# Two sums over partitions on two 32-column quarters of the PE array, in one step of a hybrid diffusion backbone

## The chip, the core and the metric

The kernel runs on one core of a Trainium2 chip. The metric is the device time of one execution in microseconds (us). A core has five engines with queues of their own: PE (TensorE, matrix products), DVE (VectorE), ACT (ScalarE), POOL (GpSimd) and SP (SyncE), which here issues every data transfer. PE loads a stationary operand (its weights, an operand in the array) and streams a moving operand past it; the result goes to PSUM, which has 128 partitions in banks of 2 KB per partition. An engine works off its queue in order, and semaphores make it wait for others.

## The reference, cut to what matters

One layer: a modulated RMSNorm, a mixer (gated DeltaNet heads beside a chunked gMLP), a gated residual, a second modulated RMSNorm, a squared-ReLU MLP, a gated residual, and a final norm. There are 128 context rows and 2048 latent rows of width 1024. The modulation is what the change touches:

```python
def modulation(cond, w_mod_l, b_mod_l):
    m = jax.nn.silu(cond) @ w_mod_l + b_mod_l          # (1,1024) @ (1024,6144) + (6144)
    return jnp.split(m[:, None, :], N_MOD, axis=-1)    # sh1, sc1, ga1, sh2, sc2, ga2
...
    mod_ctx = modulation(c_ctx[None, :], w_mod[l], b_mod[l])
...
    mod_lat = modulation(c, w_mod[l], b_mod[l])
```

So two conditioning rows (context and latent) are multiplied by the same 1024 x 6144 matrix, and the same bias row is added to both.

## The kernel before

The program is written as Python that issues instructions; a scheduler then sets the order on each engine (`schedule_with_timeline_sim=True`: it replays the program against its own cost table and picks what is ready), so an edit in one place can move instructions elsewhere. Three stages follow each other:

- Stage 1 (to about 430 us): projections of q, k and v for six blocks of tokens. Products `pj<-kH,wH`, `pj<-kL,wH` and `pj<-kH,wL` (lines 220 to 222) are one exact product in three parts of high and low halves. Transposes and small products for the scan lie between them, on the banks `pt`.
- Stage 2 (to about 1220 us): the scan over chunks in both directions, the gMLP and the output projection.
- Stage 3 (from about 1240 us to the end): the MLP, products on the banks `f`.

The modulation is worked out in twelve pieces of 512 columns. The first ones have code of their own: pieces 0 to 3 in `mod_columns`, piece 4 in `split_mod_steps`. Pieces 5 to 9 run in stage 1 and pieces 10 and 11 in stage 3, in `mod_steps(jc, ...)`, which the change edits. For each of eight chunks of 128 matrix rows it loads `raw` (128 x 512, line 235), and DVE multiplies it by the conditioning column of that chunk and adds it to an accumulator, once for each conditioning row `c` (lines 254 and 256, `acc`, in stage 3 `macc`). Then each of the two accumulators must be summed over its 128 partitions. This is `total()`: PE does it with a stationary operand `pick` that holds ones, DVE adds the bias row (line 274), and SP stores the two rows to `mod_d` in DRAM (line 275), from where later stages read them. `bias()` loads the bias (line 265).

In `total()` before, `pick` has two slices of 2 columns: a column of ones at place 0 or at place 1, zeros beside it. Both products write the same two PSUM rows, the second one onto the first.

The accumulators have one buffer each, and so has the row `mrow`: DVE can start on the next piece's `acc` only when PE has read the last one, and the bias of the next piece can be loaded only when the last row's store has landed. In stage 1 the steps of `mod_steps` are dealt out between the projections by `MOD_STEPS` and `interleave`; in stage 3 by the table `mods`.

A product of two f32 operands, such as `pm<-acc,pick`, shows in the trace as two weight loads and two matmuls: the hardware does it in two passes. A total of two products thus has four passes, and the seven totals have 28.

One other place is used in the prediction. In the scan, lines 1224 and 1228 put 64 x 64 products on quarters of the array: both contract the partitions `ra` (64 of the 128), line 1224 with its result on the partitions `ra`, line 1228 on the other 64, `rb`:

```python
T.matmul(py[ra, h, :], g["X"][ra, h, ra], pm[ra, h, 0:64], start=True, stop=True)   # L1224
...
T.matmul(px[rb, h, :], pm[ra, h, 0:64], g["X"][ra, h, ra], start=True, stop=True)   # L1228
```

On PE's queue, at the first pair of scan units (about 500 us), four of the one stand ahead of four of the other, each after its weight load:

```order
L1224 LDWEIGHTS X
L1224 MATMUL pd<-R,X 64x64
L1224 LDWEIGHTS X
L1224 MATMUL pd<-R,X 64x64
L1224 LDWEIGHTS X
L1224 MATMUL pd<-R,X 64x64
L1224 LDWEIGHTS X
L1224 MATMUL pd<-R,X 64x64
L1228 LDWEIGHTS R
L1228 MATMUL pd<-X,R 64x64
```

This place is the same in both kernels; the rows are shown because the trace has the start of each of these products.

Of the kernel before, what the change touches and what calls it, by code (L numbers as in the profile page):

```python
# [8 lines left out]
F32 = mybir.dt.float32  # L9
# [5 lines left out]
ALU = mybir.AluOpType  # L15
# [3 lines left out]
P = 128  # L19
# [43 lines left out]
def hybrid_step(  # L63
# [7 lines left out]
    V, A, G, T = nc.vector, nc.scalar, nc.gpsimd, nc.tensor  # L71
    load = nc.sync.dma_start
    store = nc.sync.dma_start
# [18 lines left out]
    mod_d = dp.tile([2, 6 * D], F32, name="mod_d")  # L92
# [73 lines left out]
    smp = ctx.enter_context(tc.tile_pool(name="small", bufs=4, reuse_waits="tile"))  # L166
# [40 lines left out]
    def w512(name, dt=F32):  # L207
        return wp.tile([P, 512], dt, tag="w", name=name)
# [12 lines left out]
            T.matmul(ps, lh, rl, start=False, stop=False, skip_group_check=more)  # L221
            T.matmul(ps, ll, rh, start=False, stop=last and i == n - 1, skip_group_check=more)  # L222

    pick = smp.tile([P, 2, 2], F32, tag="pick", name="pick", bufs=1)
    V.memset(pick, 0.0)
    V.memset(pick[:, 0, 0:1], 1.0)
    V.memset(pick[:, 1, 1:2], 1.0)

    def mod_steps(jc, pool, stage=None, psum=None, pair=None):

        u = {}

        def fetch_raw(k):
            raw = stage() if stage else sp.tile([P, 512], F32, tag="raw", name="raw")
            load(out=raw, in_=w_mod[0, k * P : (k + 1) * P, jc * 512 : (jc + 1) * 512])
            return raw

        def f(k):
            if pair:
                if k == 0:  # L240
                    u[0], u[1] = fetch_raw(0), fetch_raw(1)
                raw = u.pop(k)
                if k + 2 < KT:
                    u[k + 2] = fetch_raw(k + 2)
            else:
                raw = fetch_raw(k)
            if k == 0:
                if pair:
                    u["acc"] = pair()
                else:  # L250
                    u["acc"] = [pool.tile([P, 512], F32, tag=f"acc{c}", name="acc", bufs=1) for c in range(2)]
            for c, acc in enumerate(u["acc"]):
                if k == 0:
                    V.tensor_scalar_mul(acc, raw, scond[:, k, c : c + 1])
                else:
                    V.scalar_tensor_tensor(out=acc, in0=raw, scalar=scond[:, k, c : c + 1], in1=acc,
                                           op0=ALU.mult, op1=ALU.add)
            if k == KT - 1 and not pair:
                total()
            elif k == KT - 1:  # L260
                u["row"] = pair()[0][0:2, :]
                bias(u["row"])

        def bias(row):
            load(out=row, in_=b_mod[0:1, jc * 512 : (jc + 1) * 512].to_broadcast([2, 512]))

        def total():
            ps = (psum or pm1)()
            for c, acc in enumerate(u["acc"]):
                T.matmul(ps[0:2, :], pick[:, c, :], acc, start=c == 0, stop=c == 1)  # L270
            row = u["row"] if pair else pool.tile([2, 512], F32, tag="mrow", name="mrow", bufs=1)
            if not pair:
                bias(row)
            V.tensor_tensor(out=row, in0=ps[0:2, :], in1=row, op=ALU.add)
            store(out=mod_d[:, jc * 512 : (jc + 1) * 512], in_=row)

        return [lambda k=k: f(k) for k in range(KT)] + ([total] if pair else [])

    head = {}

    with ExitStack() as ph:
# [8 lines left out]
        def pt():  # L290
            return ppt.tile([P, 512], F32, tag="pt", name="pt", bufs=3)
# [93 lines left out]
        ps = pt()  # L385
# [328 lines left out]
        def second_mods():  # L714
# [8 lines left out]
            for cd in range(2):  # L723
                V.scalar_tensor_tensor(out=a2[:, cd, :], in0=pc4[:, cd, 1, :], scalar=1.0, in1=vec[:, 24:32],
                                       op0=ALU.add, op1=ALU.mult)

        mods = [st for jc in range(4, 10) for st in (split_mod_steps(jc) if jc == 4 else mod_steps(jc, p1))]
        blk, xs_, cols = prep_block(0)
        for st in xs_:
# [30 lines left out]
        for bi in range(len(BLOCKS)):  # L760
# [8 lines left out]
            for n, (gi, h) in enumerate(order):  # L769
                u = us[n] if bi == 0 and n < 3 else feature_tile(blk, bi, gi, h)  # L770
# [156 lines left out]
    with ExitStack() as ph:  # L927
# [554 lines left out]
        for i, u in enumerate(units):  # L1482
# [3 lines left out]
            c = i % 2  # L1486
# [107 lines left out]
    def bank():  # L1594
        return psq.tile([P, 512], F32, tag="f", name="f", bufs=8)
# [19 lines left out]
    class Unit:  # L1615
# [6 lines left out]
        def load(self, i, kh):  # L1622
            for q in range(2):
                self.raw[i, kh, q] = r = w512("raw")
                r0, c0 = kh * 512 + q * 256, self.jp * 512 + i * 256
                load(out=r.rearrange("p (a c) -> p a c", a=2),
                     in_=w_ff1[0, r0 : r0 + 256, c0 : c0 + 256].rearrange("(a p) c -> p a c", p=P))
# [130 lines left out]
    acc = {}  # L1758
# [210 lines left out]

    junk16 = smp.tile([P, 512], BF16, tag="junk16", name="junk16", bufs=1)  # L1970
    mods = [st for jc in range(10, 12) for st in mod_steps(jc, wp, lambda: w512("mraw"), bank, mrow)]
    mods = {half + 28 + 4 * j: st for j, st in enumerate(mods)}

# [8 lines left out]
    for p, (o, n, m) in enumerate(seq):  # L1982
        u = units[n]
# [37 lines left out]
    for m, (n, i, u, q) in enumerate(todo):  # L2021
# [6 lines left out]
        if q == 0:  # L2028
            ps = bank()
# [80 lines left out]
```

## Time and profile before

| | |
|---|---|
| median of 3 runs | 2579.31 us (2576.31 to 2580.29) |
| span of the profiled execution, first to last instruction | 2574.7 us (the profile gives no other time of it) |
| PE busy | 2542.1 us, 99% |
| DVE busy | 1781.9 us, 69% |
| ACT busy | 1192.5 us, 46% |
| DMA | 579.77 MB, 225 GB/s on average |

The span leaves out what lies around the execution; the median of the runs is 4.6 us longer. A profile row of a group gives the line, engine, operation, result and operands by the program's names, count, and durations in ns; a row of the timeline gives start, length, and what ran, with "x4" for four in a row. A matmul's duration in the trace includes its way through the array, and the next one starts before it ends; so what a stream of matmuls costs is read from start to start.

### The profile page before, as it was taken

What the parts mean: (1) busy time and instruction counts of PE and PEld (TensorE: products, weight loads), DVE (VectorE), ACT (ScalarE), POOL (GpSimd) and SP (SyncE); (2) the same over time, 40 slices, a digit from 0 to 9 for tenths busy, and PEclk for the clock granted to TensorE, in tenths of its full rate; (3) what the DMA queues carried; (4) which work ended last, traced back from release to release, by engine and by line L of the source; (5) the groups of instructions that cost most, each with busy time, mean ns of one, the idle gap of its engine ahead of it and who ended that gap; (6) DMA issues with size and microseconds to landing.
All of it is one profiled execution on the core that took longest, in us unless ns stands there. A gap on an engine that the chain in (4) does not pass through costs nothing.

```text
span 2574.7 us, 43713 instructions
## 1 busy us (share of the span) xinstructions
PE 2542.1 (99%) x15296; PEld 2134.4 (83%) x15296; DVE 1781.9 (69%) x3524; ACT 1192.5 (46%) x2758; POOL 313.9 (12%) x512
## 2 busy tenths in 40 slices
PE   8999999999999999999999999999999999999998
PEld 4999999788888778888888888888888888888887
DVE  5777746666667788885587887677674445675874
ACT  4755555554545556763355553333243333243441
POOL 3112112222222233331000000000000000000000
PEclk9999999999999999999999999999999999999999
DMA  8966637755555758896778798445599878786773
GB/s 293 297 221 208 197 118 231 235 165 168 165 168 177 229 185 261 280 311 209 268 219 252 214 292 284 140 144 155 177 298 310 279 261 301 238 258 212 232 251 107
DMA packets 533859, 579.77 MB, mean 225 GB/s; under 512 B 35500, under 2 KB 366684, under 8 KB 530054
## 3 DMA queue, kind: packets, MB, share of 16 engines
q1 hardware_dynamic: 533638, 576.98, 70.5%
q8 instruction: 120, 1.97, 0.3%
q14 instruction: 101, 0.83, 0.1%
HBM read 397.62 MB, written 179.22 MB: 224 GB/s over the span
## 4 chain that ended last, share of the span: by engine, by line
PE 55%; DVE 1%; issue 1%; DMA 0%; ACT 0%; POOL 0%; SPq 0%; DVEq 0%; POOLq 0%; ACTq 0%
PE f L220 17%; PE f L221 17%; PE f L222 17%; PE pj L220 1%; PE pj L222 1%; PE pj L221 1%; PE f L856 0%; PE pd L992 0%; PE pd L1096 0%; PE pd L1097 0%; DMA gr<-g_d 0%; PE pm L1418 0%; DMA x<-in_x_sample_dram 0%; PE pd L1060 0%; PE f L270 0%
## 5 line engine op out<-in xcount | busy, mean ns | idle before, releaser
L220 PE MATMUL f<-hop,zH 128*128 128x512 f32 x960 | 373.2, 389 | 0.0
L222 PE MATMUL f<-hop,zL 128*128 128x512 f32 x960 | 373.1, 389 | 0.0
L221 PE MATMUL f<-hop,zH 128*128 128x512 f32 x960 | 373.1, 389 | 0.0
L220 PE MATMUL f<-hop,wH 128*128 128x512 f32 x896 | 351.5, 393 | 0.0
L221 PE MATMUL f<-hop,wH 128*128 128x512 f32 x896 | 348.9, 390 | 0.0
L222 PE MATMUL f<-hop,wL 128*128 128x512 f32 x896 | 344.3, 390 | 0.0
L1604 ACT CAST zH<-zraw 128x512 fp32r<-128x512 f32 x240 | 146.5, 620 | 296.0 <-DMA zraw<-s_d 92.7
L1598 DVE TENSOR_TENSOR zL<-zraw,zH 128x512 fp32r<-128x512 f32 x240 | 162.1, 687 | 72.7 <-ACT zH L1604 61.6
L220 PEld LDWEIGHTS f<-hop,zH 128*128 128x128 f32 x960 | 180.3, 188 | 37.3
L222 PEld LDWEIGHTS f<-hop,zL 128*128 128x128 f32 x960 | 180.2, 188 | 37.3
L221 PEld LDWEIGHTS f<-hop,zH 128*128 128x128 f32 x960 | 180.2, 188 | 37.3
L222 PEld LDWEIGHTS f<-hop,wL 128*128 128x128 f32 x896 | 168.2, 188 | 35.6
L220 PEld LDWEIGHTS f<-hop,wH 128*128 128x128 f32 x896 | 168.5, 188 | 34.1 <-issue 0.9
L221 PEld LDWEIGHTS f<-hop,wH 128*128 128x128 f32 x896 | 168.6, 188 | 32.2
L222 PE MATMUL pj<-kH,wL 128*128 128x386 f32 (+2 forms) x568 | 190.6, 335 | 0.0
L220 PE MATMUL pj<-kH,wH 128*128 128x386 f32 (+2 forms) x568 | 189.1, 336 | 0.3 <-DVE kH L487 0.3
L221 PE MATMUL pj<-kL,wH 128*128 128x386 f32 (+2 forms) x568 | 189.3, 333 | 0.0
L178 POOL TENSOR_TENSOR r<-rsq,nhalf 128x1 f32<-128x1 f32 (+1 forms) x38 | 22.3, 587 | 1352.4 <-DVE rsq L177 1352.4
L1751 ACT CAST wH<-s 128x512 fp32r<-128x512 f32 x96 | 58.9, 620 | 172.8 <-DVE s L1598 157.3
L537 DVE SCALAR_TENSOR_TENSOR cv<-pj,vec,cv 128x384 f32<-128x384 f32 (+2 forms) x164 | 87.1, 538 | 58.4 <-ACT cv L534 57.0
L220 PEld LDWEIGHTS pj<-kH,wH 128*128 128x128 f32 x568 | 107.1, 189 | 4.9 <-issue 4.4
L221 PEld LDWEIGHTS pj<-kL,wH 128*128 128x128 f32 x568 | 107.4, 189 | 0.6
(408 smaller groups left out, 5729.3 us busy)
## 6 DMA issues: line engine op xcount, KB each, us to landing
zraw<-z_d SPq DMA_DIRECT2D x212, 256.0 KB
raw<-in_w_ff_dram SPq DMA_DIRECT2D x128, 256.0 KB
hop<-hop_d SPq DMA_DIRECT2D x28, 1024.0 KB
z_d<-c SPq DMA_DIRECT2D x96, 256.0 KB
zraw<-s_d SPq DMA_DIRECT2D x96, 256.0 KB
raw<-in_w_mod_dram SPq DMA_DIRECT2D x80, 256.0 KB
r<-in_w_ff_dram SPq DMA_DIRECT2D x80, 256.0 KB
s_d<-s SPq DMA_DIRECT2D x64, 256.0 KB
```

The source lines that it names most:

```text
L178: G.tensor_tensor(out=out, in0=t[:np_, :n], in1=nhalf[:np_, :n], op=ALU.pow)
L220: T.matmul(ps, lh, rh, start=first and i == 0, stop=False, skip_group_check=more)
L221: T.matmul(ps, lh, rl, start=False, stop=False, skip_group_check=more)
L222: T.matmul(ps, ll, rh, start=False, stop=last and i == n - 1, skip_group_check=more)
L537: V.scalar_tensor_tensor(out=cv[:, o : o + m], in0=ps[:, s + sh : s + sh + m], scalar=convw[:, w, j : j + 1], in1=cv[:, o : o + m], op0=AL ...
L1598: V.tensor_tensor(out=out, in0=a, in1=b, op=op)
L1604: A.copy(h, src)
L1751: A.copy(h, s2)
```

## The change

`pick` becomes one tile of 32 columns with ones in column 0. The two products of `total()` use the same `pick`. The one for conditioning row 0 goes to columns 0 to 31 of the array with its result on PSUM partitions 0 to 31, the other to columns 32 to 63 with its result on partitions 32 to 63, each a product of its own (`start` and `stop` both set) instead of the second being added to the first. The sums then lie on partitions 0 and 32 instead of 0 and 1, so the bias load, the bias add and the store, one instruction each before on two rows, become two each on one row.

```diff
-    pick = smp.tile([P, 2, 2], F32, tag="pick", name="pick", bufs=1)
+    pick = smp.tile([P, 32], F32, tag="pick", name="pick", bufs=1)
     V.memset(pick, 0.0)
-    V.memset(pick[:, 0, 0:1], 1.0)
-    V.memset(pick[:, 1, 1:2], 1.0)
+    V.memset(pick[:, 0:1], 1.0)
...
-                u["row"] = pair()[0][0:2, :]
+                u["row"] = pair()[0][0:33, :]
                 bias(u["row"])
 
+        def one(c):
+            return slice(32 * c, 32 * c + 1)
+
         def bias(row):
-            load(out=row, in_=b_mod[0:1, jc * 512 : (jc + 1) * 512].to_broadcast([2, 512]))
+            for c in range(2):
+                load(out=row[one(c), :], in_=b_mod[0:1, jc * 512 : (jc + 1) * 512])
 
         def total():
             ps = (psum or pm1)()
             for c, acc in enumerate(u["acc"]):
-                T.matmul(ps[0:2, :], pick[:, c, :], acc, start=c == 0, stop=c == 1)
-            row = u["row"] if pair else pool.tile([2, 512], F32, tag="mrow", name="mrow", bufs=1)
+                T.matmul(ps[32 * c : 32 * c + 32, :], pick, acc, start=True, stop=True)
+            row = u["row"] if pair else pool.tile([33, 512], F32, tag="mrow", name="mrow", bufs=1)
             if not pair:
                 bias(row)
-            V.tensor_tensor(out=row, in0=ps[0:2, :], in1=row, op=ALU.add)
-            store(out=mod_d[:, jc * 512 : (jc + 1) * 512], in_=row)
+            for c in range(2):
+                V.tensor_tensor(out=row[one(c), :], in0=ps[one(c), :], in1=row[one(c), :], op=ALU.add)
+                store(out=mod_d[c : c + 1, jc * 512 : (jc + 1) * 512], in_=row[one(c), :])
```

The scheduler's order changes with it. PE and ACT have the same instructions in both kernels; between about 150 and 360 us several hundred of them stand in another order, and after that PE's order is the same again to the end. Three places matter for the prediction (line numbers after the change are up to 4 higher below the edit: L270, L274, L275 and L265 become L273, L278, L279 and L268).

PE, the third of the five totals of stage 1. Before, it follows the second one after 282 instructions of PE:

```order
L221 MATMUL pj<-kL,wH 128x386
L222 MATMUL pj<-kH,wL 128x386
L270 MATMUL pm<-acc,pick 2x512 x2
L549 MATMUL pt<-ident,x_3215 128x128 x3
L220 MATMUL pj<-kH,wH 128x386
```

After, it stands 141 instructions behind the second one, between other projections:

```order
L583 MATMUL pt<-ident,kn 128x128 x3
L222 MATMUL pj<-kH,wL 128x386
L273 MATMUL pm<-acc,pick 32x512 x2
L220 MATMUL pj<-kH,wH 128x386
L221 MATMUL pj<-kL,wH 128x386
```

It has moved forward by half the way; its two products still stand side by side, as they do in the first, second and fourth total and in the two of stage 3.

PE, the fifth total. Before:

```order
L222 MATMUL pj<-kH,wL 128x386
L270 MATMUL pm<-acc,pick 2x512 x2
L220 MATMUL pj<-kH,wH 128x386
```

After, the first of its two products stands here:

```order
L222 MATMUL pj<-kH,wL 128x386
L273 MATMUL pm<-acc,pick 32x512
L220 MATMUL pj<-kH,wH 128x386
L221 MATMUL pj<-kL,wH 128x386
L222 MATMUL pj<-kH,wL 128x386
```

and the second one 53 instructions later:

```order
L222 MATMUL pj<-kH,wL 128x386
L273 MATMUL pm<-acc,pick 32x512
L220 MATMUL pj<-kH,wH 128x386
L221 MATMUL pj<-kL,wH 128x386
```

This is the one total whose products no longer follow each other.

SP's queue at the second total of stage 1's `mod_steps`: the store of the first total's rows and the load of the second one's bias. Before:

```order
L275 DMA mod_d<-mrow 2x512
L235 DMA raw<-in_w_mod_dram 128x512
L430 DMA x<-in_x_sample_dram 128x1024
L235 DMA raw<-in_w_mod_dram 128x512
L544 DMA qT_d<-x_2115 128x384
L593 DMA kk_d<-ev 128x3x128
L265 DMA mrow<-in_b_mod_dram 2x512
L235 DMA raw<-in_w_mod_dram 128x512
```

After:

```order
L279 DMA mod_d<-mrow 1x512 x2
L234 DMA raw<-in_w_mod_dram 128x512
L434 DMA x<-in_x_sample_dram 128x1024 x2
L268 DMA mrow<-in_b_mod_dram 1x512
L597 DMA kk_d<-ev 128x3x128
L234 DMA raw<-in_w_mod_dram 128x512
L548 DMA qT_d<-x_2114 128x384
L268 DMA mrow<-in_b_mod_dram 1x512
L234 DMA raw<-in_w_mod_dram 128x512
```

A store and a load more stand in the queue, ahead of loads of `raw` (the matrix chunks) and of `x` (the tokens).

## Prediction

> **What bounds the kernel now.** I read the page's head, its busy row, the slices and the chain first:
>
> ```profile
> span 2574.7 us, 43713 instructions
> PE 2542.1 (99%) x15296; PEld 2134.4 (83%) x15296; DVE 1781.9 (69%) x3524; ACT 1192.5 (46%) x2758; POOL 313.9 (12%) x512
> PE   8999999999999999999999999999999999999998
> PEclk9999999999999999999999999999999999999999
> PE 55%; DVE 1%; issue 1%; DMA 0%; ACT 0%; POOL 0%; SPq 0%; DVEq 0%; POOLq 0%; ACTq 0%
> ```
>
> PE is busy nearly all the time at a granted clock of nine tenths or more, and the chain that ended last runs over PE wherever it can be named. The totals lie in three stretches, so I asked for the engines' busy time there (columns: window, then busy us and instructions of PE, weight loads, DVE, ACT, POOL, then clock and DMA):
>
> ```profile
> 140.00:360.00 220.00, 220.00 (x1321) 207.83 (x1320) 151.42 (x290) 118.96 (x368) 39.52 (x114) 1.00 0.63 199
> 1715.00:1730.00 15.00, 15.00 (x66) 11.03 (x65) 12.13 (x20) 2.84 (x5) 0.00 (x0) 1.00 0.31 89
> 1820.00:1830.00 10.00, 10.00 (x46) 7.00 (x45) 9.28 (x16) 3.25 (x6) 0.00 (x0) 1.00 0.73 214
> ```
>
> PE has no gap in any of them. So a microsecond that PE saves in a total should come off the end, and work added to DVE, ACT or SP costs nothing until it makes PE wait.
>
> **What a total costs now.** PE's timeline around the first one, then its weight loads, then PE around the first one of stage 3:
>
> ```profile
> 152.09 0.34 PE L221 MATMUL pj<-kL,wH 128*128 128x386 f32 x1
> 152.27 0.33 PE L222 MATMUL pj<-kH,wL 128*128 128x386 f32 x1
> 152.53 1.88 PE L270 MATMUL pm<-acc,pick 128*2 128x512 f32 x4
> 154.34 0.44 PE L220 MATMUL pj<-kH,wH 128*128 128x386 f32 x1
> 154.62 0.34 PE L221 MATMUL pj<-kL,wH 128*128 128x386 f32 x1
> 154.80 0.34 PE L222 MATMUL pj<-kH,wL 128*128 128x386 f32 x1
> ...
> 152.97 0.08 PEld L270 LDWEIGHTS pm<-acc,pick 128*2 128x2 f32 x1 [0.34 <-issue]
> 153.39 0.09 PEld L270 LDWEIGHTS pm<-acc,pick 128*2 128x2 f32 x1 [0.34 <-issue]
> ...
> 1721.08 0.39 PE L222 MATMUL f<-hop,wL 128*128 128x512 f32 x1
> 1721.39 1.88 PE L270 MATMUL f<-macc,pick 128*2 128x512 f32 x4
> 1723.20 0.50 PE L220 MATMUL f<-hop,wH 128*128 128x512 f32 x1
> 1723.54 0.39 PE L221 MATMUL f<-hop,wH 128*128 128x512 f32 x1
> 1723.77 0.40 PE L222 MATMUL f<-hop,wL 128*128 128x512 f32 x1
> ```
>
> From the start of L222 at 152.27 to that of L221 at 154.62 are 2.35 us; without the total two ordinary steps of 0.18 (152.09 to 152.27, 154.62 to 154.80) would lie there. So a total costs 1.99, and by the same count 2.46 less two steps of 0.23, or 2.00, in stage 3. I take 2.00. The passes start 0.43 apart (the weight loads at 152.53, 152.97, 153.39), four of them make 1.72, and the other 0.28 is the border: the step into this shape of the array and out of it. All seven are alike:
>
> ```profile
> L270 PE MATMUL pm<-acc,pick x20: 591/592/592, 152.5 to 347.8; 128*2 128x512 f32 x20
> L270 PE MATMUL f<-macc,pick x8: 591/592/592, 1721.4 to 1826.0; 128*2 128x512 f32 x8
> ```
>
> That is 28 passes, 7 x 2.00 = 14.0 us in all, of which nothing more than half can be had by running the products two at a time.
>
> **Whether two products share the array.** The trace before has no product on a 32-column quarter beside another. Nearest to it are lines 1224 and 1228 of the scan, two products from the same 64 partitions into different halves of the columns. On the queue four of the one stand ahead of four of the other; PE's timeline has their starts as
>
> ```profile
> 500.46 0.21 PE L1224 MATMUL pd<-R,X 64*64 64x64 f16 x1
> 500.48 0.21 PE L1228 MATMUL pd<-X,R 64*64 64x64 f16 x1
> 500.52 0.19 PE L1224 MATMUL pd<-R,X 64*64 64x64 f16 x1
> 500.53 0.19 PE L1228 MATMUL pd<-X,R 64*64 64x64 f16 x1
> 500.55 0.19 PE L1224 MATMUL pd<-R,X 64*64 64x64 f16 x1
> 500.56 0.19 PE L1228 MATMUL pd<-X,R 64*64 64x64 f16 x1
> 500.58 0.19 PE L1224 MATMUL pd<-R,X 64*64 64x64 f16 x1
> 500.59 0.19 PE L1228 MATMUL pd<-X,R 64*64 64x64 f16 x1
> ...
> 538.75 0.34 PE L1224 MATMUL pd<-R,X 64*64 64x64 f16 x5
> 538.90 0.21 PE L1228 MATMUL pd<-X,R 64*64 64x64 f16 x1
> ```
>
> The first L1228 starts 0.02 after the first L1224 and before the second one, though it is fifth on the queue: the two parts of the array work side by side, each at its own pace of 0.03. At 538.75, where both directions agree and eight of each stand in line, the first L1228 comes after five of L1224, so PE reaches only a few products past one that is held up. A total needs less: two passes of the first product, then two of the second.
>
> Bounds for one total whose products follow each other: with full overlap two passes of 0.43 in each quarter, 0.02 apart, and the border, 0.86 + 0.02 + 0.28 = 1.16, a gain of 0.84. With none 2.00, a gain of nothing. If each change of quarter costs a border of its own, a loss of 0.28. I take the gain, by the nearest row, and keep the others for the range.
>
> The Trainium skill says otherwise in "TensorE: Matmul & The Clock Gate", section "Part 3: Packing small matmuls — row/col tiling": matmuls are strictly first in, first out, and only weight loads are pulled ahead. The rows at 500.46 do not agree, L1228 is ahead of three of L1224 there. By that rule the time would be 2577.0, as the first rival works out. The same section gives 2.38x for three column tiles; if two lost the same share they would reach about 1.6x, an estimate by which a total would gain about 0.64 instead of 0.84 and the time would be 2575.7.
>
> **The change part by part.**
>
> - Six totals (the first four of stage 1, the two of stage 3) keep their products side by side: 6 x 0.84 = 5.04 us off PE.
> - The fifth total is torn apart by the scheduler, 53 instructions between its halves. Nothing is there to share the array with, and the border is paid twice: +0.28.
> - The weights have 32 columns instead of 2. The load of a pass starts while the pass before streams (152.97, 153.39) and has 0.43 to hide in. Nothing, even if it took three times as long as its 0.08 to 0.09.
> - Seven more bias adds on DVE, seven more loads and seven more stores on SP. Their rows:
>
> ```profile
> L274 DVE TENSOR_TENSOR mrow<-pm,mrow x5: 668/672/679, 155.2 to 348.4; 2x512 f32<-2x512 f32 x5
> L265 SPq DMA_DIRECT2D mrow<-in_b_mod_dram x5: 261/261/424, 126.0 to 305.5; - x5
> L275 SPq DMA_DIRECT2D mod_d<-mrow x5: 248/253/262, 156.3 to 349.1; - x5
> SPq L265 <- DMA mod_d<-mrow: 2.0, 3, 1.2
> L256 DVE SCALAR_TENSOR_TENSOR acc<-raw,scond,acc 128x512 f32<-128x512 f32 x56 | 39.6, 738 | 0.7 <-DMA raw<-in_w_mod_dram 0.6
> ```
>
>   The add has as many elements per partition as before, so each takes 0.67 again: 7 x 0.67 = 4.7 us on DVE, five of them in the window with 220 - 151 = 69 us to spare. On SP 7 x (0.26 + 0.25) = 3.6 us of issue. The bias load waits for the last store to land (2.0 us in three waits), and the loads of `raw` and `x` behind it wait with it; now two loads do so, the second about a quarter of a microsecond longer. What hides all this is that DVE waited only 0.6 us for `raw` in that window. If that cover went, DVE would start some accumulations late, and PE would feel it only through a projection bank not yet emptied. I cost it at nothing.
> - The order. PE has the same work between 150 and 360 us and no gap there, so a shuffle can win next to nothing and loses only by a new wait. The third total, near 250 us now (the middle of 152.5 and 347.8), comes about 25 us earlier (141 instead of 282 instructions behind the second, 0.18 each), and with it the accumulation of the fourth piece. I take nothing, with 1.5 us either way: a little over 1.2, the longest single wait in the rows above, should one such wait reach PE or leave it.
> - `pick` is filled by two small memsets instead of three, at the start, while PE waits for loads: nothing.
>
> Sum: -5.04 + 0.28 = -4.76 us against the profiled span of 2574.7, which gives 2569.9. The median of the runs stands 4.6 above that span, 2579.31, so the time forecast is 2574.5.
>
> **The rivals.**
>
> - *In queue order.* PE starts no product ahead of one that stands before it, so the second product's first pass lies only beside the first one's second pass: three passes' time instead of four, a gain of 0.43 in six totals, 2.58 - 0.28 = 2.30, time 2577.0. Against it stands 500.46, for it that those were f16 products of 64 columns without two passes per product.
> - *No overlap.* Quarters of an f32 product with all 128 partitions in use may not share the stream at all: +0.28, time 2579.6. Each pass reads 512 columns in 0.43, while the projections' 512-column passes start 0.23 apart, so one f32 stream leaves half of that pace; that speaks against.
> - *A border at each change of quarter.* 6 x 0.28 + 0.28 = +1.96, time 2581.3. The change of half at 500.46 cost 0.02.
> - *DVE held up by an early fourth piece* (the other side). With the third total about 25 us earlier, DVE begins the fourth piece near 225 instead of 250 us, and its first chunks must be there:
>
> ```profile
> L235 SPq DMA_DIRECT2D raw<-in_w_mod_dram x8: 328/392/803, 203.1 to 220.4; - x8
> ```
>
>   The last of the early ones is issued at 220.4, so some 5 us are left for it to land where some 30 were. DVE takes its work in order: if it waits, the convolutions behind it are late, projection banks stay full, and PE stops. Two banks beyond the one in use cover about 8 us (24 products of 0.18 fill one). The time ends above that of before once DVE is later than that cover and the 4.76 together, about 13 us; at 20 us late it would be 2574.5 + 12, about 2586. DVE's 69 idle us in this stretch speak against.
>
> **How the numbers follow.** Two kernels are told apart here from about 0.2%, 5.2 us (the three runs span 4 us). Full overlap 0.66, in queue order 0.11, no overlap 0.14, borders 0.05, DVE held up 0.04. Full overlap with 1.5 us of order and 1 us of scatter each way reaches from 2571.5 to 2577; its 4.76 is just short of 5.2, so 0.30 of its 0.66 fall under faster and 0.36 under same. The second, third and fourth case are all same (0.30), the last is slower, and I put 0.02 from the same with it for an unlucky order: faster 0.30, same 0.64, slower 0.06. The range takes in the borders' case, 2571.5 to 2581.3.
>
> **What would show it.** In the profile after: the two products of a total with starts about 0.02 apart and the next projection about 0.94 after the first of them instead of 1.81; the fifth total as two pairs of passes; DVE's bias adds 14 of 0.67; PE without a gap from 140 to 360 us. The forecast is wrong if the second product starts 0.43 or 0.86 behind the first, or if PE shows waits for DVE or ACT in projections between 200 and 360 us.

## The result, and the profile after

The changed kernel took 2589.34 us (median of 5 runs, 2588.96 to 2591.48), the kernel before on the same chip 2578.51. The ratio is 1.0047, with a 95% interval of 1.0036 to 1.0058: about 10.8 us slower, where 4.8 us faster was forecast. The profiled execution took 2589.02 us, of which the span is 2587.0.

The head of the page of the changed kernel, its busy row, PE's slices and clock, and the chain that ended last:

```profile
span 2587.0 us, 43751 instructions
PE 2552.9 (99%) x15296; PEld 2135.1 (83%) x15296; DVE 1787.9 (69%) x3530; ACT 1192.8 (46%) x2758; POOL 316.3 (12%) x512
PE   8999999999999999999999999999999999999998
PEclk9999999999999999999999999999999999999999
PE 60%; DVE 3%; DMA 1%; issue 1%; ACT 1%; POOL 0%; SPq 0%; DVEq 0%; POOLq 0%; ACTq 0%
```

The span is 12.3 us longer, and PE's busy time 10.8 us, with the same 15296 matmuls at the same clock, and the chain still runs over PE. So PE's waits account for only 1.5 us of the 12.3 (the span less the busy time, 34.1 against 32.6): for the most part, the same products took longer.

The totals are not where it went. PE's timeline of the changed kernel around the first total, the first half of the fifth one, and the first total of stage 3:

```profile
152.78 0.33 PE L222 MATMUL pj<-kH,wL 128*128 128x386 f32 x1
153.04 1.05 PE L273 MATMUL pm<-acc,pick 128*32 128x512 f32 x4
154.02 0.45 PE L220 MATMUL pj<-kH,wH 128*128 128x386 f32 x1
154.31 0.34 PE L221 MATMUL pj<-kL,wH 128*128 128x386 f32 x1
...
319.17 0.34 PE L222 MATMUL pj<-kH,wL 128*128 128x386 f32 x1
319.44 1.04 PE L273 MATMUL pm<-acc,pick 128*32 128x512 f32 x2
320.42 0.45 PE L220 MATMUL pj<-kH,wH 128*128 128x386 f32 x1
320.70 0.34 PE L221 MATMUL pj<-kL,wH 128*128 128x386 f32 x1
...
1724.15 0.39 PE L222 MATMUL f<-hop,wL 128*128 128x512 f32 x1
1724.47 1.05 PE L273 MATMUL f<-macc,pick 128*32 128x512 f32 x4
1725.45 0.50 PE L220 MATMUL f<-hop,wH 128*128 128x512 f32 x1
1725.79 0.39 PE L221 MATMUL f<-hop,wH 128*128 128x512 f32 x1
```

Counted as in the prediction, the first total costs 154.31 - 152.78 - 2 x 0.18 = 1.17 us (forecast 1.16), the one in stage 3 1725.79 - 1724.15 - 2 x 0.23 = 1.18. One product alone, the half at 319.44 with two passes ("x2"), costs 320.70 - 319.17 - 0.36 = 1.17 as well: the second product beside the first costs nothing that can be seen. In the record of each start the two products of the first total begin at 153.038 and 153.044, their second passes at 153.491 and 153.498.

The other rows that the prediction named, by source line, and the engines' window of stage 1:

```profile
L273 PEld LDWEIGHTS pm<-acc,pick x20: 106/108/109, 153.0 to 329.4; 128*32 128x32 f32 x20
L278 DVE TENSOR_TENSOR mrow<-pm,mrow x10: 668/680/683, 155.2 to 331.2; 1x512 f32<-1x512 f32 x10
L278 DVE TENSOR_TENSOR macc<-f,macc x4: 672/678/684, 1726.4 to 1830.1; 1x512 f32<-1x512 f32 x4
140.00:360.00 220.00, 220.00 (x1342) 210.31 (x1341) 156.08 (x296) 122.02 (x378) 41.96 (x114) 1.00 0.63 200
```

The loads of 32 columns take 0.11 us, there are 14 bias adds of 0.67 to 0.68, and PE has no gap from 140 to 360 us. All as forecast.

The loss is in the MLP, which the diff doesn't touch. The costliest group of the page, before and then after, and how many matmuls PE started in the same 100 us, before and then after:

```profile
L220 PE MATMUL f<-hop,zH 128*128 128x512 f32 x960 | 373.2, 389 | 0.0
```

```profile
L220 PE MATMUL f<-hop,zH 128*128 128x512 f32 x960 | 376.5, 392 | 0.0
```

```profile
2000.00:2100.00 100.00, 100.00 (x443) 82.84 (x442) 52.92 (x81) 42.38 (x75) 0.00 (x0) 1.00 0.87 296
```

```profile
2000.00:2100.00 100.00, 100.00 (x436) 81.58 (x435) 49.89 (x77) 39.19 (x68) 0.00 (x0) 1.00 0.84 294
```

The clock is 1.00 in both, PE is full in both, and there are 436 products instead of 443. PE's timeline of the changed kernel shows two paces next to each other:

```profile
1990.05 0.39 PE L221 MATMUL f<-hop,zH 128*128 128x512 f32 x1
...
1992.77 0.39 PE L221 MATMUL f<-hop,zH 128*128 128x512 f32 x1
1992.99 0.39 PE L222 MATMUL f<-hop,zL 128*128 128x512 f32 x1
1993.22 0.40 PE L220 MATMUL f<-hop,zH 128*128 128x512 f32 x1
...
1995.32 0.39 PE L220 MATMUL f<-hop,zH 128*128 128x512 f32 x1
```

From 1990.05 to 1992.77 are 12 steps in 2.72 us, 227 ns each; from 1993.22 to 1995.32 are 9 in 2.10, 233 ns each. The kernel before has 227 on both sides of that place; behind it, nine steps take 2.04 us:

```profile
1993.10 0.39 PE L221 MATMUL f<-hop,zH 128*128 128x512 f32 x1
...
1995.14 0.39 PE L221 MATMUL f<-hop,zH 128*128 128x512 f32 x1
```

The border between the paces is where the streamed operand, `hop`, changes from a tile of one pool to a tile of another. `hop_tile` takes them from the pool `hopB` or from `hopA`. The stationary operands of the MLP (`wH`, `wL`, `zH`, `zL`) all lie in the pool `wp`. Here and below, the pace of a pool is the median time that twelve steps in a row take while `hop` comes from that pool, divided by twelve. It is 226.7 ns before for both pools; after, it is 226.7 for `hopB` and 234.3 for `hopA`. DVE, ACT and the transfers don't make the difference: during 356 of the steps on `hopA` neither DVE nor ACT was busy, and they took 234.0 ns on average (before: 332 steps, 226.7); during 43 of these no DMA packet was under way either, 234.3 (before: 38 steps, 226.7). 1992 of the 5568 products of 512 columns stream from `hopA`: 1992 x 7.6 ns = 15.1 us, an estimate of the loss.

What has moved is the place of tiles in SBUF. `pick` lies in the small pool ahead of `wp`. Before, it took 16 bytes per partition in a slot of 32; after, it takes 128. Everything allocated behind it, `wp` and `hopB` among it, lies 96 bytes higher. `hopA` is allocated from the other end (`side="right"`) and has stayed. In the built programs `hopA` begins 182784 bytes behind `wp` before, which is 714 x 256, and 182688 after, 96 short of that.

To see all of the time by place, the table takes PE's matmuls by their number on PE's queue and gives the us between the same two of them (columns: the first total's start; stage 1 from about there; the rest of stage 1 and stage 2, up to the MLP's first product; the MLP up to the totals in it; the two totals, each with six products before and six behind it; the MLP between them and after them).

| kernel | first total at | stage 1 | to the MLP | MLP, first part | totals | MLP, the rest |
|---|---|---|---|---|---|---|
| before | 152.54 | 238.37 | 849.87 | 479.97 | 4.75 + 4.08 | 98.57 + 737.41 |
| after | 153.04 | 235.39 | 851.63 | 483.76 | 3.93 + 3.30 | 99.08 + 747.57 |
| difference | +0.50 | -2.98 | +1.76 | +3.79 | -1.60 | +10.67 |

The sum is +12.1 of the 12.3. The totals gained 2.98 + 1.60 = 4.58 us, and the MLP lost 14.5, in all of its parts. (The 1.76 lies within what this stretch shows in the other kernels below, 849.18 to 852.63.)

### The profile page after: what moved, and what is told of

It is laid out like the page before. It is cut to its first block, busy times and chain, and to the rows that moved or that the text cites. A ratio compares the mean times of both kernels' runs of the same rounds, so it can differ in the third digit from the quotient of the medians.

```text
span 2587.0 us, 43751 instructions
## 1 busy us (share of the span) xinstructions
PE 2552.9 (99%) x15296; PEld 2135.1 (83%) x15296; DVE 1787.9 (69%) x3530; ACT 1192.8 (46%) x2758; POOL 316.3 (12%) x512
## 4 chain that ended last, share of the span: by engine, by line
PE 60%; DVE 3%; DMA 1%; issue 1%; ACT 1%; POOL 0%; SPq 0%; DVEq 0%; POOLq 0%; ACTq 0%
PE f L220 17%; PE f L221 17%; PE f L222 17%; PE pj L220 1%; PE pj L221 1%; PE pj L222 1%; PE pd L996 1%; PE pd L1100 1%; PE pd L1101 1%; PE pm L1422 0%; PE pd L1064 0%; PE pd L1191 0%; DVE x L853 0%; PE f L860 0%; DVE vt L1058 0%
```

## The experiments

The theory at the outset: the place of the MLP's operands in SBUF sets the pace, and the totals gained what was forecast. The rival: something else in the change slows PE from about 1240 us on.

**Experiments 1 to 4: move pools and nothing else.** Experiment 1 is the changed kernel with a `pick` of 40 columns, of which 32 are used:

```diff
-    pick = smp.tile([P, 32], F32, tag="pick", name="pick", bufs=1)
+    pick = smp.tile([P, 40], F32, tag="pick", name="pick", bufs=1)[:, 0:32]
```

> The changed kernel with the tile of pick 160 bytes long instead of 128 (its last 32 bytes unused), so that the pools behind it lie 32 bytes further on and start at multiples of 64 again, as before the change; instructions and their order as in the changed kernel. Layout theory (MLP products that stream from the pool hopA, which did not move, against weights from the pool wp, which the change moved by 96 bytes, start 234 ns apart instead of 227): 227 in all of them, 1992 products give back 13.4 us, 2589.3 - 13.4 = 2575.9. Order theory (the scheduler's new order and the extra loads, stores and adds cost the time): nothing changes, 2589.

Experiment 2 is the kernel before with a `pick` of 48 bytes in place of 16, of which 16 are used, so that what lies behind it moves up by 32:

```diff
-    pick = smp.tile([P, 2, 2], F32, tag="pick", name="pick", bufs=1)
+    pick = smp.tile([P, 12], F32, tag="pick", name="pick", bufs=1)[:, 0:4].rearrange("p (a b) -> p a b", a=2)
```

> The kernel before with the tile of pick 48 bytes long instead of 16, which moves the pools behind it by 32 bytes; instructions and order as before. Layout theory: the products that stream from hopA start 234 ns apart, 13.4 us more, 2578.5 + 13.4 = 2591.9. Order theory: no change, 2578.5.

Experiments 3 and 4 move `hopA` instead. `zcol`, a tile of zeros, lies at the right edge, and with eight columns more `hopA` begins 32 bytes lower, while `wp` stays. Experiment 3 is the changed kernel with this edit, experiment 4 the kernel before with it:

```diff
-    zcol = edge.tile([P, 3 * KT], F32, name="zcol")[:, 0:KT]
+    zcol = edge.tile([P, 3 * KT + 8], F32, name="zcol")[:, 0:KT]
```

> The changed kernel with 32 unused bytes added to the tile zcol at the far end of the memory, so that hopA moves too, by 32 bytes, and streamed and stationary operands again differ by a multiple of 64, both 32 bytes off one. If the distance of the two operands counts: 227 ns, 2575.9. If each operand's own place against multiples of 64 counts: no gain, 2589 or more. Order theory: 2589.

> The kernel before with the same 32 bytes at zcol: hopA lies 32 bytes off a multiple of 64, wp on one. If the distance counts, or the streamed operand's own place: 234 ns in the 1992 products that stream from hopA, 2578.5 + 13.4 = 2591.9. If only the place of the weights counts: 227 ns, 2578.5. Order theory: 2578.5.

| | wp to hopA, bytes short of a multiple of 256 | median us | against before (2577.17), 95% | pace hopA / hopB, ns |
|---|---|---|---|---|
| 1, after | 128 | 2585.77 | 1.0030 (1.0019 to 1.0042) | 233.3 / 226.7 |
| 2, before | 32 | 2592.78 | 1.0057 (1.0044 to 1.0071) | 233.3 / 226.7 |
| 3, after | 128 | 2587.51 | 1.0037 (1.0023 to 1.0050) | 233.3 / 226.7 |
| 4, before | 32 | 2592.20 | 1.0057 (1.0042 to 1.0072) | 233.3 / 226.7 |

The spans of experiments 2 and 4 and their costliest groups, each pair from its page:

```profile
span 2589.1 us, 43713 instructions
...
L220 PE MATMUL f<-hop,zH 128*128 128x512 f32 x960 | 376.6, 393 | 0.0
```

```profile
span 2587.9 us, 43713 instructions
...
L220 PE MATMUL f<-hop,zH 128*128 128x512 f32 x960 | 376.5, 393 | 0.0
```

Both are the kernel before, with its two-column products one after the other, and 32 bytes that nobody reads make it 0.57% slower. So a loss of this kind needs nothing of the change but the bytes. Experiments 2 and 4 move different pools and have the same distance between `wp` and `hopA`, and the same pace; so do 1 and 3. That points at the distance and not at the place of either pool. All four are slow, so what is left for the rival is tested by experiments 5 and 6.

Experiments 1 and 3 missed what the theory expected of them. A step of 64 was assumed, and with it the old pace of 227 ns; but 128 bytes short, the pace was 233.3. The row of experiment 1, for comparison:

```profile
L220 PE MATMUL f<-hop,zH 128*128 128x512 f32 x960 | 375.7, 392 | 0.0
```

**Experiments 5 to 7: the distance restored, and its step.** Experiment 5 is the changed kernel with its `pick`, and with the small pool shrunk elsewhere by as much (the tag `c16` gets two buffers in place of the pool's default of four), so that all pools behind it lie where they lay before:

```diff
-    pick = smp.tile([P, 32], F32, tag="pick", name="pick", bufs=1)
+    pick = smp.tile([P, 40], F32, tag="pick", name="pick", bufs=1)[:, 0:32]
...
-        cvec = smp.tile([P, 16], F32, tag="c16", name="cvec")
+        cvec = smp.tile([P, 16], F32, tag="c16", name="cvec", bufs=2)
...
-        st_ = smp.tile([P, 16], F32, tag="c16", name="c16")
+        st_ = smp.tile([P, 16], F32, tag="c16", name="c16", bufs=2)
```

> The changed kernel with every pool at exactly the place that it has in the kernel before (the tile of pick 160 bytes long, and another small tile with two buffers instead of four, which it has no more use for); instructions and their order as in the changed kernel. The last runs left this: with the padding by 32 bytes the distance from wp to hopA is 128 bytes short of that before (182656 against 182784), and the same distance gave the same pace whichever of the two was moved. Distance theory: at 182784 again the 1992 products that stream from hopA start 227 ns apart, and only the totals' gain is left, six times 0.84 less 0.28: 4.8 below the kernel before, 2577.2 - 4.8 = 2572.4. Rival (something else in the changed kernel, its order or the new loads and stores, costs what is left in the padded one): about 2585.8 as with the padding.

Experiment 6 goes the other way, up to the next multiple of 256, with a `pick` of 72 columns of which 32 are used:

```diff
-    pick = smp.tile([P, 32], F32, tag="pick", name="pick", bufs=1)
+    pick = smp.tile([P, 72], F32, tag="pick", name="pick", bufs=1)[:, 0:32]
```

> The changed kernel with the tile of pick 288 bytes long: wp and the pools behind it lie 256 bytes further on than before, the distance to hopA is 182528, 256 above a multiple of 512. If the pace depends on the distance modulo 256 or less: 227 ns and 2572.4. If modulo 512 or more: 232 to 234 ns and about 2586.

Experiment 7 is the kernel before with 64 bytes more, as experiment 2 has 32:

```diff
-    pick = smp.tile([P, 2, 2], F32, tag="pick", name="pick", bufs=1)
+    pick = smp.tile([P, 24], F32, tag="pick", name="pick", bufs=1)[:, 0:4].rearrange("p (a b) -> p a b", a=2)
```

> The kernel before with the tile of pick 80 bytes longer, so that wp moves by 64 bytes and the distance to hopA is 182720, 64 short of that before. Distance theory: not the old distance modulo 256 or 512, so 232 to 235 ns and about 2577.2 + 14 = 2591. If multiples of 64 were harmless and something else made the padded changed kernel slow: 2577.2.

| | bytes short | median us | against before (2577.05), 95% | pace hopA, ns |
|---|---|---|---|---|
| 5, after | 0 | 2572.46 | 0.9984 (0.9975 to 0.9993) | 226.7 |
| 6, after | 256 | 2573.17 | 0.9985 (0.9976 to 0.9994) | 226.7 |
| 7, before | 64 | 2591.78 | 1.0055 (1.0039 to 1.0070) | 233.3 |

The page of experiment 5, and its window in the MLP, which has 443 products again:

```profile
span 2572.3 us, 43751 instructions
...
L220 PE MATMUL f<-hop,zH 128*128 128x512 f32 x960 | 373.2, 389 | 0.0
```

```profile
2000.00:2100.00 100.00, 100.00 (x443) 82.80 (x442) 51.33 (x78) 42.31 (x74) 0.00 (x0) 1.00 0.81 280
```

With the tiles where they were, the change is worth what it was forecast to be worth: 4.6 us between the medians, 1.8 to 6.4 by the interval. Nothing is left for the rival: the order, the loads, stores and adds of the change are all in this kernel. Experiment 6 has all pools behind `pick` at another place and the same time, so not the old place is good but a distance that is a multiple of 256. 32, 64, 96 and 128 bytes short of it are all slow, 233.3 or 234.3 ns. Over its three parts the MLP took 14.5 us more than before at 96 bytes short, 13.7 to 13.8 at 32 and 64, 12.2 and 12.6 at 128, and from 0.1 less to 0.5 more in experiments 5 and 6.

**Experiment 8: no overlap, with the good distance.** The changed kernel with one stationary operand of 33 columns per product, so that it covers two quarters of the array and the products must follow each other; the doubled adds, loads and stores stay. Its third total is torn apart, where the changed kernel's fifth one is:

```diff
-    pick = smp.tile([P, 32], F32, tag="pick", name="pick", bufs=1)
+    pick = smp.tile([P, 72], F32, tag="pick", name="pick", bufs=1)[:, 0:65]
     V.memset(pick, 0.0)
-    V.memset(pick[:, 0:1], 1.0)
+    V.memset(pick[:, 32:33], 1.0)
...
-                T.matmul(ps[32 * c : 32 * c + 32, :], pick, acc, start=True, stop=True)
+                T.matmul(ps[0:33, :], pick[:, 32 - 32 * c : 65 - 32 * c], acc, start=c == 0, stop=c == 1)
```

> The overlap alone undone, with the pools 256 bytes on as in the padding by 160 bytes, where the MLP ran at 227 ns: pick has 65 columns with ones in column 32, and both products of a total go to the same half of the array with 33 columns, one added onto the other, results on partitions 0 and 32 as in the changed kernel; the bias loads, adds and stores stay doubled. The scheduler orders it much like the changed kernel, with the third total torn apart instead of the fifth. If overlap is what the change gains and the doubled small work is free: four passes in line again, six totals at 2.00 and one at 2.28, 2577.1 + 0.3 = 2577.4. If the gain of the last two runs came from the new order: 2572 to 2573. If the doubled loads, adds and stores cost time: above 2578.

It took 2578.69, the kernel before 2579.1 on the same chip, ratio 1.0001 (0.9992 to 1.0010). PE's timeline around its first total:

```profile
153.14 0.33 PE L222 MATMUL pj<-kH,wL 128*128 128x386 f32 x1
153.40 1.91 PE L273 MATMUL pm<-acc,pick 128*33 128x512 f32 x4
155.23 0.45 PE L220 MATMUL pj<-kH,wH 128*128 128x386 f32 x1
```

The next projection comes 1.83 after the first pass, as it did before the change (1.81), instead of 0.98. Between the same products as in the table above, stage 1 takes 238.89 and the two totals 4.78 and 4.11, against 235.44, 3.93 and 3.25 in experiment 6: 5.16 us. So the overlap is the whole gain, and the doubled small work on DVE and SP costs nothing that shows within the interval, 0.1% each way. The three times in the expectation were worked out from 2577.1 for the kernel before; on this chip it took 2579.1, so they move up by 2.0, and 2578.69 lies with the first case (2579.4), not with the third (above 2580).

**Experiment 9: spoil the other pool.** If the distance to the stationary operand is what counts, `hopB` must slow down alone when it alone is moved. The kernel before with 32 unused bytes ahead of `hopB`; `wp` and `hopA` stay:

```diff
+    gap = ctx.enter_context(tc.tile_pool(name="gap", bufs=1))
+    gap.tile([P, 8], F32, name="gap")
     hops["B"] = ctx.enter_context(tc.tile_pool(name="hopB", bufs=1, reuse_waits="tile"))
```

> The kernel before with 32 unused bytes ahead of the pool hopB, from which the other three fifths of the MLP's products stream; hopA and wp stay. Instructions and order as before. Distance theory: hopA's 1992 products stay at 227 ns, hopB's 3576 go to 233 or 234, about 6.7 ns each or 24 us more, 2601; by the scale of the 15 us that 1992 cost when hopA was moved, 2604. If only hopA has a place that matters: 2577.1.

It took 2603.0, against 2579.1 before, ratio 1.0095 (1.0082 to 1.0109), with 226.7 ns for `hopA` and 233.3 for `hopB`, which now begins 32 bytes past a multiple of 256 from `wp`. Its span, costliest group and window:

```profile
span 2598.1 us, 43713 instructions
...
L220 PE MATMUL f<-hop,zH 128*128 128x512 f32 x960 | 378.3, 394 | 0.0
```

```profile
2000.00:2100.00 100.00, 100.00 (x435) 81.27 (x434) 45.69 (x69) 36.07 (x62) 0.00 (x0) 1.00 0.85 293
```

The MLP's three parts took 488.50, 100.11 and 752.05 us, 24.7 more than before, over the other 3576 products: 6.9 ns each. The two pools have changed roles. Thirty-two bytes that nothing reads cost 24 us.

## Why the prediction was wrong

The forecast was 2574.5 us and 0.94 for no slower; it came out at 2589.34, above the whole range.

- *The step that failed* is the bullet on `pick`: "is filled by two small memsets instead of three, at the start, while PE waits for loads: nothing". It priced the tile's instructions and not its bytes. The diff has the larger tile in its first two lines, and the 96 bytes it adds move `wp` against `hopA`. The runs give that step +14.5 us in the MLP's parts, three times the whole gain. No rival had it either, since all of them looked for the cost at the totals or in stage 1. The trace of before has no row that shows this price: both pools stood at the good distance there and ran at the same 227 ns.
- *Six totals side by side, 0.84 each*: right. Measured 2.00 - 1.17 = 0.83 in stage 1, 0.82 and 0.81 in stage 3. Experiment 8 takes it away and gives 5.16 us back, against 5.04 forecast.
- *The fifth total, +0.28*: nearly. Each half costs about 1.17, so 2.34 instead of 2.00, +0.34; 4 x 0.83 - 0.34 = 2.98 is what stage 1 gained.
- *In queue order*: not so. The second product's first pass starts 0.006 us behind the first one's and 0.45 ahead of the first product's second pass. If the two passes of a product follow each other on the queue, as the prediction took it (the trace doesn't name them), PE doesn't work off its queue strictly in order; the rows at 500.46 show the same without that condition. The Trainium skill's rule of strict first in, first out for matmuls ("TensorE: Matmul & The Clock Gate", section "Part 3: Packing small matmuls — row/col tiling") does not agree with these starts. The share of two column tiles that was estimated from its 2.38x does not either: two products cost what one costs.
- *No overlap, and a border at each change of quarter*: excluded by the same starts, and by experiment 8 for what no overlap would be.
- *DVE held up by an early fourth piece*: the kernel did get slower, but not this way. The third total came 26 us earlier, PE shows no gap from 140 to 360 us, and stage 1 got shorter.
- *Seven more adds, loads and stores, the weights of 32 columns, the order, at nothing*: right. Experiment 8 has them all without the gain and stands at 1.0001 (0.9992 to 1.0010). The order cost nothing in stage 1, where the sum comes out without it.

So the sum was right for what it listed, -4.76 forecast against -4.58 at the totals, and experiment 5 at 2572.46 lies in the range of the likeliest case. What was missing was a term.

## What to carry to other kernels

A tile that changes its size moves every tile behind it: list where the operands of the hottest products lie before and after the edit, also for products that the edit doesn't touch, and price the move as a term of its own. Here a distance between the streamed and the stationary tile that was a multiple of 256 bytes per partition gave 226.7 ns for a product of 512 columns, and every other one tried 233.3 or 234.3. When a local change moves the time by more than it can hold, count the matmuls in equal windows far away from it: 443 against 436 in 100 us, at a full PE and the same clock, showed the place within one view.

## What the runs showed of the hardware

In the MLP, PE's pace depended on the distance in SBUF between the pool of the stationary operands and the pool of the streamed ones. It was 226.7 ns per product at multiples of 256 bytes (three of them: `hopA` in the kernel before, `hopA` in experiment 6, `hopB`), 233.3 at 32, 64 and 128 short and 234.3 at 96 short. Both pools showed it (experiments 2 and 9), and kernels with and without the change. The weight loads themselves kept their duration, a median of 187 or 188 ns in each of these kernels.

Which reads get in each other's way is open. PE loads the next stationary tile while it streams the present operand (in the changed kernel, the load for the product that starts at 1992.09 starts at 1991.86, with the product before it), and the slow pace was there with DVE, ACT and the transfers idle too, so these two are the nearest suspects. The Trainium skill says in "TensorE: Matmul & The Clock Gate", section "Part 2: What happens when you issue a matmul", that there are two independent read ports and that loading the next weights takes no bandwidth from the running matmul. By that rule the distance should not matter. If these two reads are what collides, the 3% in the pace does not agree with the rule; but no run here separates the weight load from the stream. Streams without a weight load between them were not tried, and neither were distances that are no multiple of 32. The 386-column products of stage 1 showed nothing of it. By the tiles' places in the built program of the kernel before, about half of line 220's products there stream at a distance of a multiple of 256 and half 128 beside one; the median step to the next product was 175 ns in both halves.

A pair of f32 products on two 32-column quarters cost 1.17 us and one alone 1.17: two products at the price of one, each of two passes, at 128 partitions and 512 columns. The steps into this shape of the array and out of it are in both, and a torn pair pays them twice (2.34 for the fifth total).
